# Layer 0's first shift columns: x loaded first, and four K tiles on TensorE instead of two there and two on VectorE

## Chip, cores and metric

The kernel runs on one core of a Trainium2 chip. The metric is the device time of one execution in microseconds (us), the median of several runs. The engines are TensorE (PE in the profile, its weight loads PEld), VectorE (DVE), ScalarE (ACT), GpSimd (POOL) and SyncE (SP), whose queue issues most of the loads.

## What is computed

Two blocks of two layers each, on x of 256 rows and 2048 columns, all in float32. The change is in the very beginning of layer 0 of the first block:

```python
mod = jax.nn.silu(c) @ w_mod + b_mod          # c: 2048, w_mod: 2048 x 6144
shift, scale, gate = jnp.split(mod, 3, axis=-1)
h = rms_norm(x, g_pre) * (1.0 + scale[:, None, :]) + shift[:, None, :]
proj = h @ w_in
```

Behind it come mixers (window attention, spatial gating, gated linear attention), the output projection, and a second block with attention and an MLP. None of that is touched.

## The kernel before

The 2048 columns of x are 16 K tiles of 128. The projection `h @ w_in` of layer 0 runs in four phases of four K tiles each, so that phase 0 can begin when scale and shift of only K tiles 0 to 3 are known; those of later K tiles come as background work on VectorE during the phase ahead. The diff is in the code that makes scale and shift for K tiles 0 to 3, ahead of phase 0. Everything there is the prologue.

There are two ways of multiplying the vector sc = silu(c) with a piece of w_mod. `gemv` (L488 to L501) loads tiles of 128 x 1024 (`raw`, two rows of K by 512 columns, or four by 256), scales each piece by one column of sc and adds it into `gacc` on VectorE (the first step is L494, the others L496), and at the end sums gacc over its 128 partitions with one matmul against a column of ones for each K tile (L501). `gemv_pe` (L522, L526) loads 128 x 8 x 128 tiles and multiplies on TensorE: for each K tile of the result two raw tiles and 16 matmuls with a 128 x 128 weight load and one moving column. All raw tiles come from one ring of five buffers, which the tiles of w_in use as well, so a load waits until the tile five places ahead has been used up. `mod_done` (L510, L512) adds the bias, and for the scale the gain.

In source order the kernel begins with four steps of the scale's gemv and four of gemv_pe for the shift of K tiles 0 and 1, one after the other, then transposes small vectors (`fill_fm`, L173), runs the rest of the scale, loads x (`x_load`, L154), squares it on ScalarE (`x_done`, L390), and runs gemv for the shift of K tiles 2 and 3. `block1` then makes 1/rms (L239, POOL L241, ACT L770, PE L771, copy L773), transposes x (L750), multiplies with scale (L754, VectorE) and adds the shift: the hi part of h is written by L762 on ScalarE and its remainder by L763 on VectorE; K tile 3 is kept whole by L758. Each weight tile of w_in is split the same way (L265 on ScalarE makes hi, L266 on VectorE makes lo), and TensorE multiplies three times (L287, L288, L289), or once where the K tile is whole (L325).

The order in which each engine gets its instructions is not the source's: the framework that builds the program interleaves independent work. Each engine then works through its own list in order, and one instruction that waits holds up all behind it. Where an instruction stands is therefore read from the built program.

Of the kernel before, what the change touches and what calls it, by code (L numbers as in the profile page):

```python
# [11 lines left out]
F32 = mybir.dt.float32  # L12
# [9 lines left out]
P = 128  # L22
S = 256
D = 2048
KT = D // P
# [65 lines left out]
def kernel(  # L91
# [7 lines left out]
    V, A, PE, G = nc.vector, nc.scalar, nc.tensor, nc.gpsimd  # L99

    const = ctx.enter_context(tc.tile_pool(name="const", bufs=1))
# [14 lines left out]
    def tm(tag, shape=(P, 512), dt=F32):  # L116
        return ring.tile(list(shape), dt, tag=tag, bufs=BUFS[tag], name=f"{tag}{next(uid)}")
# [10 lines left out]
    def gate_load(t, on):  # L128

        V.tensor_copy(out=t[0:1, 0:1], in_=on)  # L130

    def bank(pool=None, shape=(P, 512)):
        pool = pool or aux
        return pool.tile(list(shape), F32, tag="b", name=f"b{next(uid)}")
# [13 lines left out]
    def x_load(src, on=None):  # L148
        for n in range(4):
            for t in range(2):  # L150
                X[t][n] = tm("act")
                if on is not None:
                    gate_load(X[t][n], on)
                nc.sync.dma_start(out=X[t][n], in_=src[t * P:(t + 1) * P, n * 512:(n + 1) * 512])  # L154
# [25 lines left out]
    def fill_fm(on):  # L180
        fm_load(1, [both("bmod", b_mod), both("gpre", g_pre)], on)
        fm_load(2, [both("gpost", g_post), both("an", attn_norm_2), both("mn", mlp_norm_2), both("qn", q_a_norm_2),
                    both("kvn", kv_a_norm_2)], on)
# [75 lines left out]
    def raw_tile(tag="raw"):  # L259
        return wp.tile([P, 1024], F32, tag=tag, bufs={"raw": 5, "rawm": 2}[tag], name=f"{tag}{next(uid)}")  # L260
# [33 lines left out]
    def settle(age=0):  # L294

        while late and bg["n"] - late[0][0] >= age:
            late.pop(0)[1]()
# [87 lines left out]
    def x_done(t, n):  # L385

        if n == 0:
            ssx[t] = small(4)
        j = junk
        A.activation(out=j, in_=X[t][n], func=AF.Square, accum_out=ssx[t][:, n:n + 1])  # L390
# [82 lines left out]
    mod = {}  # L473
    idle = itertools.cycle(["k", "pT", "k", "s"])

    def gemv(l, part, k0, nk, eng, tag, into=None):

        if (l, part) not in mod:
            mod[l, part] = const.tile([P, KT], F32, name=f"mod{l}_{part}")
        n = nk * P  # L480
        per = 1024 // n
        if tag == "idle":
            per = 1
        n0 = part * D + k0 * P
        acc = gacc.tile([P, 1024], F32, tag="gacc", name=f"gacc{next(uid)}")[:, :n]
        for u in range(0, KT, per):
            raw = tm(next(idle)) if tag == "idle" else raw_tile(tag)
            nc.sync.dma_start(  # L488
                out=raw[:, :per * n].rearrange("p (k n) -> p k n", k=per),
                in_=w_mod[l, u * P:(u + per) * P, n0:n0 + n].rearrange("(k p) n -> p k n", p=P))  # L490
            for k in range(per):
                w = raw[:, k * n:(k + 1) * n]
                if u + k == 0:
                    eng.tensor_scalar(out=acc, in0=w, scalar1=sc[:, 0:1], scalar2=None, op0=MUL)  # L494
                else:
                    eng.scalar_tensor_tensor(out=acc, in0=w, scalar=sc[:, u + k:u + k + 1], in1=acc, op0=MUL, op1=ADD)  # L496
            if u + per == KT:
                def finish():
                    pb = bank(fin) if into is None else into
                    for i in range(nk):  # L500
                        PE.matmul(pb[:, i:i + 1], lhsT=acc[:, i * P:(i + 1) * P], rhs=ones[:, 0:1],  # L501
                                  start=True, stop=True)
                    if into is None:
                        mod_done(l, part, k0, nk, pb)
                late.append((bg["n"], finish))
            yield

    def mod_done(l, part, k0, nk, pb):
        o = mod[l, part][:, k0:k0 + nk]
        V.tensor_tensor(out=o, in0=pb[:, :nk], in1=fv(("bmod", l), part * KT + k0, nk), op=ADD)  # L510
        if part == 1:
            V.scalar_tensor_tensor(out=o, in0=o, scalar=1.0, in1=fv(("gpre", l), k0, nk), op0=ADD, op1=MUL)  # L512
        elif part == 2:
            V.tensor_tensor(out=o, in0=o, in1=fv(("gpost", l), k0, nk), op=MUL)

    def gemv_pe(l, part, k0, nk, tag, pb):

        for i in range(nk):
            n0 = part * D + (k0 + i) * P
            for u in range(0, KT, 8):  # L520
                raw = raw_tile(tag)
                nc.sync.dma_start(  # L522
                    out=raw.rearrange("p (k n) -> p k n", k=8),
                    in_=w_mod[l, u * P:(u + 8) * P, n0:n0 + P].rearrange("(k p) n -> p k n", p=P))
                for k in range(8):
                    PE.matmul(pb[:, i:i + 1], lhsT=raw[:, k * P:(k + 1) * P], rhs=sc[:, u + k:u + k + 1],  # L526
                              start=(u + k == 0), stop=(u + k == KT - 1))
                yield
# [726 lines left out]
    def mods(l, part, *ranges, eng=V, tag="rawm"):  # L1255
        return [gemv(l, part, k0, nk, eng, tag) for k0, nk in ranges]

    def run(gens):
        for g in gens:
            for _ in g:  # L1260
                pass
        settle()
# [25 lines left out]
    UN0 = 9  # L1288
    UN1 = 24
    RATE1 = 48  # L1290
    NPE = 2
    RATE0 = 31
    SPLIT0 = ("q0", "q1", "kv", "z0", "z1", "su", "sv", "z3", "qk", "v0", "v1")
    WHOLE0 = (3, 7, 11, 14, 15)
    pb = bank()
    scale, shift = mods(0, 1, (0, 4), tag="raw")[0], gemv_pe(0, 0, 0, NPE, "raw", pb)
    for i in range(4):
        next(scale)
        next(shift, None)
    fill_fm(None)  # L1300
    run([scale])
    x_load(x[0])
    for n in range(4):
        for t in range(2):
            x_done(t, n)
    run([gemv(0, 0, NPE, 4 - NPE, V, "raw", pb[:, NPE:])])
    mod_done(0, 0, 0, 4, pb)
    mask1 = const.tile([P, 512], F32, tag="mask", name="mask1")[:, :S]
    nc.gpsimd.dma_start(out=mask1, in_=cst[:, C_SWA:C_SWA + S])
    if N1:  # L1310
        block1(0, [(0,), (4,), (8,), (12,)], SPLIT0, ORDER, prepare0, lambda: None, WHOLE0)
    if N1 > 1:
# [61 lines left out]
```

## Time and profile before

| | us |
|---|---|
| median of 3 runs | 3034.97 (3031.36 to 3038.36) |
| profiled execution | 3032.83 |
| its span, first to last instruction | 3031.1 |
| TensorE busy in the span | 2944.8 |
| VectorE busy | 1985.4 |
| ScalarE busy | 1439.4 |
| first projection matmul (L287) starts | 50.31 |

The profile is one execution. A row of its timeline has the start, the length and the engine of a run of like instructions, with xN for N records. The profile records each float32 matmul of the prologue twice, so that the eight matmuls of one `gemv_pe` tile are x16. A matmul group's mean duration is longer than the pace at which they follow each other, because they overlap; so a run is read by its length, not by count times mean.

### The profile page before, as it was taken

The numbers are of one execution on the slowest core, as the hardware profiler recorded it, in microseconds if no ns is written. First come the engines' busy times: TensorE is split into PE (matmuls) and PEld (weight loads), VectorE is DVE, ScalarE is ACT, GpSimd is POOL, SyncE is SP. The second block draws the span as 40 slices with busy tenths as digits, with TensorE's granted clock in tenths as the row PEclk, the third lists the DMA queues.
The fourth block names the chain that finished last, engine by engine and source line by source line (L and its number), as shares of the span: only waits on it lengthen the run. The fifth ranks groups of instructions, "written<-read, shape, count | busy, mean of one in ns | idle before, by whom it ended". The sixth has DMA issues, their size and how long they took to land.

```text
span 3031.1 us, 40011 instructions
## 1 busy us (share of the span) xinstructions
PE 2944.8 (97%) x15002; PEld 2437.6 (80%) x15002; DVE 1985.4 (66%) x2832; ACT 1439.4 (47%) x2273; POOL 37.5 (1%) x56
## 2 busy tenths in 40 slices
PE   6999998999999999999999999999999999999998
PEld 5776676778787887888888888888788888888887
DVE  6898877678866565565666655665555655656655
ACT  2334545445556555544444444455554444444444
POOL 0000000000000000000000000000000000000000
PEclk9999998999999999999999999999999999999999
DMA  9998678888455555566666666554556666656664
GB/s 296 331 305 298 186 262 268 289 278 280 134 180 143 178 146 171 181 188 191 191 189 189 191 189 190 190 173 134 167 170 201 192 189 188 192 189 190 189 191 153
DMA packets 318838, 617.55 MB, mean 204 GB/s; under 512 B 21000, under 2 KB 48836, under 8 KB 318644
## 3 DMA queue, kind: packets, MB, share of 16 engines
q1 hardware_dynamic: 317988, 614.40, 64.2%
q8 instruction: 117, 1.92, 0.3%
q0 software_dynamic: 336, 0.49, 0.1%
q14 instruction: 77, 0.63, 0.1%
q10 hardware_dynamic: 320, 0.12, 0.0%
HBM read 610.73 MB, written 4.19 MB: 203 GB/s over the span
## 4 chain that ended last, share of the span: by engine, by line
PE 86%; DMA 6%; DVE 5%; ACT 2%; issue 1%; POOL 0%; SPq 0%; ACTq 0%; POOLq 0%; DVEq 0%
PE b L288 17%; PE b L289 17%; PE b L287 17%; PE b L1193 16%; PE b L1195 8%; DMA rawm<-in_w_mod_dram 4%; PE b L325 2%; DVE gacc L496 1%; PE b L366 1%; DVE lo L266 1%; PE b L567 1%; ACT hi L265 1%; PE b L554 1%; PE b L955 1%; PE b L501 0%
## 5 line engine op out<-in xcount | busy, mean ns | idle before, releaser
L266 DVE TENSOR_TENSOR lo<-raw,hi 128x1024 fp32r<-128x1024 f32 (+4 forms) x964 | 1126.2, 1170 | 798.2 <-ACT hi L265 794.8
L265 ACT CAST hi<-raw 128x1024 fp32r<-128x1024 f32 (+4 forms) x964 | 972.8, 1010 | 1284.8 <-PE b L289 783.8
L287 PE MATMUL b<-hi,act 128*128 128x512 f32 (+2 forms) x2728 | 1074.1, 394 | 4.6 <-ACT hi L265 2.2
L288 PE MATMUL b<-lo,act 128*128 128x512 f32 (+2 forms) x2728 | 1048.4, 384 | 8.7 <-DVE lo L266 8.7
L289 PE MATMUL b<-hi,act 128*128 128x512 f32 (+2 forms) x2728 | 1044.2, 383 | 0.4 <-DVE act L252 0.4
L1193 PE MATMUL b<-act,hi 128*128 128x512 f32 x2048 | 721.0, 397 | 0.0
L288 PEld LDWEIGHTS b<-lo,act 128*128 128x128 f32 x2728 | 515.7, 189 | 119.7 <-DVE lo L266 14.3
L287 PEld LDWEIGHTS b<-hi,act 128*128 128x128 f32 x2728 | 515.5, 189 | 115.1 <-issue 14.9
L289 PEld LDWEIGHTS b<-hi,act 128*128 128x128 f32 x2728 | 515.2, 189 | 97.3 <-issue 0.8
L1195 PE MATMUL b<-act,lo 128*128 128x256 f32 x2048 | 574.9, 281 | 0.0
L1193 PEld LDWEIGHTS b<-act,hi 128*128 128x128 f32 x2048 | 384.4, 188 | 92.7
L1195 PEld LDWEIGHTS b<-act,lo 128*128 128x128 f32 x2048 | 386.9, 189 | 0.5
L496 DVE SCALAR_TENSOR_TENSOR gacc<-rawm,sc,gacc 128x1024 f32<-128x1024 f32 x120 | 153.6, 1280 | 51.6 <-DMA rawm<-in_w_mod_dram 51.4
L325 PE MATMUL b<-raw,act 128*128 128x512 f32 (+1 forms) x240 | 110.3, 559 | 0.0
L1211 DVE SCALAR_TENSOR_TENSOR act<-b,s,act 128x512 f32<-128x512 f32 x128 | 90.0, 743 | 5.7 <-PE b L289 5.7
L354 ACT ACTIVATE s<-s,s 128x128 f32<-128x128 f32 (+3 forms) x144 | 64.1, 447 | 38.9 <-DVE s L351 37.8
L241 POOL TENSOR_TENSOR s<-s,cs 128x1 f32<-128x1 f32 (+1 forms) x38 | 28.6, 755 | 2892.7 <-DVE s L239 2806.0
L325 PEld LDWEIGHTS b<-raw,act 128*128 128x128 f32 x240 | 43.4, 189 | 17.9 <-issue 12.0
L1203 DVE SCALAR_TENSOR_TENSOR h<-h 128x256 f32<-128x256 f32 x128 | 54.5, 426 | 4.4
L390 ACT ACTIVATE junk<-act 128x512 bf16<-128x512 f32 x56 | 35.0, 626 | 42.8 <-DMA act<-in_x_dram 22.8
L824 DVE TENSOR_TENSOR act<-b,act 128x512 f32<-128x512 f32 (+2 forms) x82 | 51.5, 631 | 5.9 <-PE b L325 4.9
L1201 DVE TENSOR_TENSOR h<-b,h 128x256 f32<-128x256 f32 x128 | 53.4, 417 | 0.0
(272 smaller groups left out, 1725.9 us busy)
## 6 DMA issues: line engine op xcount, KB each, us to landing
raw<-in_w_in_dram SPq DMA_DIRECT2D x256, 512.0 KB, 4.7
raw<-in_w_up_dram SPq DMA_DIRECT2D x256, 512.0 KB, 3.7
raw<-in_w_down_dram SPq DMA_DIRECT2D x256, 512.0 KB, 3.6
rawm<-in_w_mod_dram SPq DMA_DIRECT2D x128, 512.0 KB, 4.8
raw<-in_w_out_dram SPq DMA_DIRECT2D x64, 512.0 KB, 4.8
raw<-in_w_o_dram SPq DMA_DIRECT2D x64, 512.0 KB, 3.7
k<-in_w_mod_dram SPq DMA_DIRECT2D x48, 256.0 KB, 4.9
raw<-in_w_in_dram SPq DMA_DIRECT2D x32, 288.0 KB, 2.9
```

The source lines that it names most:

```text
L265: A.copy(out=hi[:, :n], in_=src)
L266: V.tensor_tensor(out=lo[:, :n], in0=src, in1=hi[:, :n].bitcast(F32), op=SUB)
L287: PE.matmul(ps, lhsT=xa, rhs=wh, start=first, stop=False)
L288: PE.matmul(ps, lhsT=xa, rhs=wl, start=False, stop=False)
L289: PE.matmul(ps, lhsT=xb, rhs=wh, start=False, stop=last)
L325: PE.matmul(ps[t][:, :n], lhsT=a[:, t * P:(t + 1) * P], rhs=wh, start=kk + j == units[0], stop=kk + j == units[-1] + 3)
L354: A.activation(out=s[:, h, :], in_=s[:, h, :], func=AF.Exp, bias=nm[:, h:h + 1], accum_out=den[:, h:h + 1])
L496: eng.scalar_tensor_tensor(out=acc, in0=w, scalar=sc[:, u + k:u + k + 1], in1=acc, op0=MUL, op1=ADD)
L1193: PE.matmul(ps[f], lhsT=wh[:, f * P:(f + 1) * P], rhs=a.rearrange("p a b -> p (a b)"), start=(kk + j == 0), stop=False)
L1195: PE.matmul(ps[f][:, S:], lhsT=wl[:, f * P:(f + 1) * P], rhs=a[:, 0, :], start=False, stop=(kk + j == KT - 1))
L1203: V.scalar_tensor_tensor(out=s2, in0=s, scalar=0.0, in1=s, op0=MAX, op1=MUL)
L1211: V.scalar_tensor_tensor(out=xc, in0=ps, scalar=r2[t], in1=xc, op0=MUL, op1=ADD)
```

## The change

x_load goes to the front of SyncE's queue. The scale's gemv is no longer interleaved with gemv_pe, and stands whole behind fill_fm. The shift of all four K tiles is made by gemv_pe, behind the scale in the source, and the gemv of K tiles 2 and 3 is gone.

```diff
-    NPE = 2
     RATE0 = 31
...
+    x_load(x[0])
     pb = bank()
-    scale, shift = mods(0, 1, (0, 4), tag="raw")[0], gemv_pe(0, 0, 0, NPE, "raw", pb)
-    for i in range(4):
-        next(scale)
-        next(shift, None)
     fill_fm(None)
-    run([scale])
-    x_load(x[0])
+    run(mods(0, 1, (0, 4), tag="raw"))
     for n in range(4):
         for t in range(2):
             x_done(t, n)
-    run([gemv(0, 0, NPE, 4 - NPE, V, "raw", pb[:, NPE:])])
+    run([gemv_pe(0, 0, 0, 4, "raw", pb)])
+    if (0, 0) not in mod:
+        mod[0, 0] = const.tile([P, KT], F32, name="mod0_0")
     mod_done(0, 0, 0, 4, pb)
```

On TensorE the list of the kernel before begins with these rows (raw are the weight tiles, gacc the scale's sum, act the tiles of x):

```order
L526 MATMUL b_101<-sc,raw_108 128x1 x8
L173 MATMUL b_163<-cs,y_160 128x128
L173 MATMUL b_172<-cs,y_166 128x104
L526 MATMUL b_101<-sc,raw_122 128x1 x8
L526 MATMUL b_101<-sc,raw_136 128x1 x8
L526 MATMUL b_101<-sc,raw_150 128x1 x8
L750 MATMUL b_276<-cs,act_198 128x128
L501 MATMUL b_191<-cs,gacc_103 128x1 x4
```

All four L526 tiles stand ahead of L501. In the changed kernel the same place reads:

```order
L501 MATMUL b_167<-cs,gacc_134 128x1 x4
L526 MATMUL b_117<-sc,raw_184 128x1 x8
L771 MATMUL b_280<-h_281,cs 128x128
L771 MATMUL b_280<-h_284,cs 128x128
...
L526 MATMUL b_117<-sc,raw_214 128x1 x8
L526 MATMUL b_117<-sc,raw_224 128x1 x8
L526 MATMUL b_117<-sc,raw_234 128x1 x8
L526 MATMUL b_117<-sc,raw_244 128x1 x8
L526 MATMUL b_117<-sc,raw_254 128x1 x8
```

All eight tiles now stand behind L501; in the rows left out are two more of them, raw_194 and raw_204, and L750, L425 and L208. L501 itself still waits for the last VectorE step of the scale.

On ScalarE the list of the kernel before has, at the end of the prologue (mod_0 is the shift):

```order
L770 ACTIVATE h_271<-cs,s_265 128x128
L265 CAST hi_309<-raw_307 128x1024
L265 CAST hi_327<-raw_325 128x512
L265 CAST hi_357<-raw_355 128x1024
L762 ACTIVATE act_283<-h_281,mod_0_224 128x256
L762 ACTIVATE act_288<-h_286,mod_0_224 128x256
```

and the changed kernel:

```order
L770 ACTIVATE h_284<-cs,s_278 128x128
L762 ACTIVATE act_296<-h_294,mod_0_264 128x256
L762 ACTIVATE act_301<-h_299,mod_0_264 128x256
L762 ACTIVATE act_311<-h_309,mod_0_264 128x256
L758 ACTIVATE act_316<-h_314,mod_0_264 128x256
L265 CAST hi_322<-raw_320 128x1024
```

The casts of the first weight tiles moved from ahead of the instructions that wait for mod_0 to behind them. On VectorE the list of the kernel before has around mod_0 (gacc_339 is background work for the next phase):

```order
L494 TENSOR_SCALAR gacc_339<-k_340,sc 128x512
L496 SCALAR_TENSOR_TENSOR gacc_225<-raw_244,sc,gacc_225 128x256
L496 SCALAR_TENSOR_TENSOR gacc_339<-pT_343,sc,gacc_339 128x512
L496 SCALAR_TENSOR_TENSOR gacc_225<-raw_244,sc,gacc_225 128x256
L496 SCALAR_TENSOR_TENSOR gacc_339<-k_346,sc,gacc_339 128x512
L510 TENSOR_TENSOR mod_0_224<-b_101,fm 128x4
L266 TENSOR_TENSOR lo_358<-raw_355,hi_357 128x1024
```

and the changed kernel:

```order
L510 TENSOR_TENSOR mod_0_264<-b_117,fm 128x4
L763 SCALAR_TENSOR_TENSOR act_296<-h_294,mod_0_264,act_296 128x256
L763 SCALAR_TENSOR_TENSOR act_301<-h_299,mod_0_264,act_301 128x256
L763 SCALAR_TENSOR_TENSOR act_311<-h_309,mod_0_264,act_311 128x256
L266 TENSOR_TENSOR lo_323<-raw_320,hi_322 128x1024
L266 TENSOR_TENSOR lo_341<-raw_338,hi_340 128x512
L494 TENSOR_SCALAR gacc_352<-k_353,sc 128x512
```

The sixteen steps of the shift (here gacc_225) are gone, and the first splits and the first background steps moved from ahead of mod_0's L510 to behind it.

## Rows read from the trace of the kernel before

**Rows 1.** The page: busy time of TensorE, and its busy tenths in 40 slices.
```profile
PE 2944.8 (97%) x15002; PEld 2437.6 (80%) x15002; DVE 1985.4 (66%) x2832; ACT 1439.4 (47%) x2273; POOL 37.5 (1%) x56
...
PE   6999998999999999999999999999999999999998
```

**Rows 2.** Windows: start:end length, busy time by engine, granted clock, DMA share, GB/s.
```profile
0.00:10.00 10.00, 0.26 (x1) 0.18 (x1) 1.54 (x4) 1.50 (x2) 2.50 (x8) 1.00 0.76 202
10.00:20.00 10.00, 9.68 (x46) 9.62 (x46) 4.26 (x8) 0.00 (x0) 0.51 (x1) 1.00 0.89 274
20.00:30.00 10.00, 5.71 (x26) 5.34 (x27) 6.63 (x9) 1.44 (x4) 0.00 (x0) 1.00 0.97 327
30.00:40.00 10.00, 4.71 (x19) 3.59 (x19) 4.45 (x16) 5.14 (x14) 1.18 (x2) 1.00 1.05 346
40.00:50.00 10.00, 3.68 (x15) 3.13 (x16) 9.45 (x22) 3.18 (x5) 0.00 (x0) 1.00 1.01 350
...
50.00:90.00 40.00, 40.00 (x172) 30.32 (x171) 31.92 (x55) 17.71 (x33) 0.00 (x0) 1.00 0.90 310
```

**Rows 3.** Timeline 0 to 32: start, length, engine, line, tiles, records [idle before].
```profile
10.07 3.54 PE L526 MATMUL b<-sc,raw 128*128 128x1 f32 x16 [5.65 <-DMA raw<-in_w_mod_dram]
...
13.64 0.37 SPq L522 DMA_DIRECT2D raw<-in_w_mod_dram  x1
...
17.60 6.99 PE L526 MATMUL b<-sc,raw 128*128 128x1 f32 x32 [0.25 <-DMA raw<-in_w_mod_dram]
...
23.03 6.26 DVE L496 SCALAR_TENSOR_TENSOR gacc<-raw,sc,gacc 128x512 f32<-128x512 f32 x8 [2.41 <-DMA raw<-in_w_mod_dram]
...
29.35 1.87 PE L501 MATMUL b<-cs,gacc 128*128 128x1 f32 x8 [0.80 <-DVE gacc L496]
```

**Rows 4.** Timeline 40 to 52: the first cast, mod_0 and the first projection matmul.
```profile
40.95 1.05 ACT L265 CAST hi<-raw 128x1024 fp32r<-128x1024 f32 x1 [4.56 <-DMA raw<-in_w_in_dram]
...
43.76 1.22 DVE L266 TENSOR_TENSOR lo<-raw,hi 128x1024 fp32r<-128x1024 f32 x1
...
48.28 1.01 PE L501 MATMUL b<-cs,gacc 128*128 128x1 f32 x4 [4.94 <-DVE gacc L496]
...
49.33 0.16 DVE L510 TENSOR_TENSOR mod<-b,fm 128x4 f32<-128x4 f32 x1 [0.45 <-PE b L501]
...
49.53 1.31 ACT L762 ACTIVATE act<-h,mod 128x256 fp32r<-128x256 f32 x3 [2.02 <-DVE mod L510]
...
50.31 0.78 PE L287 MATMUL b<-hi,act 128*128 128x512 f32 x1
...
50.74 0.49 ACT L758 ACTIVATE act<-h,mod 128x256 f32<-128x256 f32 x1
...
51.31 0.63 PE L287 MATMUL b<-hi,act 128*128 128x512 f32 x1
...
51.74 0.63 PE L289 MATMUL b<-hi,act 128*128 128x512 f32 x1
```

**Rows 5.** Groups by line and form, 0 to 51 or 55: busy, mean ns, idle before.
```profile
L526 PE MATMUL b<-sc,raw 128*128 128x1 f32 x64 | 14.0, 351 | 5.9 <-DMA raw<-in_w_mod_dram 5.9
...
L496 DVE SCALAR_TENSOR_TENSOR gacc<-raw,sc,gacc 128x256 f32<-128x256 f32 x15 | 7.2, 480 | 0.1
L750 PE MATMUL b<-cs,act 128*128 128x128 f32 x20 | 5.5, 431 | 3.9 <-DMA act<-in_x_dram 3.5 <-DVE mod L510 0.3 <-DVE sgb L209 0.2
...
L771 PE MATMUL b<-h,cs 128*128 128x128 f32 x4 | 1.6, 502 | 3.7 <-ACT h L770 3.7
```

**Rows 6.** Timeline at 140 us: an L501 of four K tiles between projection matmuls.
```profile
140.26 0.95 PE L501 MATMUL b<-cs,gacc 128*128 128x1 f32 x8
```

**Rows 7.** The raw tiles up to 50 us: duration ns min/median/max, first and last start.
```profile
L526 PEld LDWEIGHTS b<-sc,raw x64: 288/333/338, 10.0 to 24.2; 128*128 128x128 f32 x64
```

**Rows 8.** A window at the end of a phase, columns as in rows 2.
```profile
140.00:150.00 10.00, 8.72 (x50) 7.07 (x49) 8.64 (x18) 3.33 (x4) 0.00 (x0) 1.00 0.84 271
```

## The prediction

> **What bounds the kernel now.** I read first the busy time of each engine and the span in slices: TensorE is busy 97% of the span, and of the 40 slices only the first falls clearly under nine tenths [rows 1]. So over most of the span nothing but fewer TensorE seconds helps, and the change touches none of those; what it can move is the first slice. The windows over that slice say where its idle time is: TensorE works 0.26, 9.68, 5.71, 4.71 and 3.68 us in the five stretches of 10 us up to 50, and 40.00 of 40 from 50 to 90 [rows 2]. The change therefore moves one number, the moment at which the first projection matmul (L287) starts. It starts at 50.31 us [rows 4], and a shift of it should pass to the end nearly whole, because behind it TensorE hardly waits for anything that could soak it up.
>
> What ends that prologue is read from the timeline. VectorE finishes the scale half at 29.29 (the run of eight L496 that starts at 23.03 and takes 6.26), and L501 folds it at 29.35 [rows 3]. The shift of K tiles 2 and 3 is then worked off on VectorE: sixteen steps, of which the 15 L496 of the 256-column form take 7.2 us [rows 5], spread over 35 to 48 between other work; L501 folds them at 48.28, L510 makes mod_0 at 49.33, ScalarE makes the first h tile from 49.53, and L287 follows [rows 4]. The four tiles of shift that TensorE computes (L526) run from 10.07 to 24.6, wholly beside the loads and VectorE work of the scale half [rows 3]: today they cost nothing.
>
> **What the change takes away.** The sixteen VectorE steps and the L501 of 1.01 us behind them go. In windows 30 to 50 VectorE was busy 4.45 and 9.45 us of ten [rows 2]; that is relief on the chain that ends the prologue now.
>
> **What it adds.** Eight tiles of L526 instead of four. The program's tile is eight matmuls, which the profile records as 16 rows; one tile took 3.54 us, the two that run back to back 6.99, and all four 14.0 of busy time [rows 3, 5]. So 3.50 us a tile, 28.0 us for eight.
>
> **What it moves, and this decides.** In the order of the changed program all eight tiles stand on TensorE behind the L501 of the scale half. L501 waits for the whole scale half, so none of the 28.0 us can run beside it any more; what cost nothing is now in line. The cover is lost, and nothing new covers it: between the eight tiles stand only L771, the L750 transposes and the three little transposes, and they add to the line too.
>
> **The sum.** When does L501 start? The bytes ahead of the last scale tile are the same as before: 2.1 MB of shift tiles were ahead of it, now 2.1 MB of x, with 4.2 MB of scale. So it is not later than 29.35 [rows 3]. The gain is that SyncE's queue no longer stands still for TensorE's tiles (the transfer issued at 13.64 is one that waited until the first L526 tile was done [rows 3]). At the highest rate of the prologue, 350 GB/s [rows 2], 6.3 MB take 18.0 us, and with the first issue at 1.7 and one last pair of steps of 1.57 (6.26 / 4) that is 21.3 at the earliest. At the rates that the windows had, 202 then 274 then 327 GB/s, 2.0 MB are in by 10, 4.8 MB by 20 and 6.3 MB by 24.7, plus 1.57: 26.3. I take 26.3, since these are this program's own rates at its start. From there, in program order on TensorE: L501 1.87 [rows 3] gives 28.2; eight tiles 28.0 give 56.2; L771 1.6 [rows 5] gives 57.8; twelve of the L750 stand in the line (four are ahead of L501, four beside the work behind mod_0) and three smaller transposes, fifteen at the 5.5 / 20 = 0.275 of an L750 [rows 5], 4.1, gives 61.9. Then 0.20 to mod_0, as between the end of L501 at 49.29 and that of L510 at 49.49 [rows 4]: 62.1.
>
> Behind mod_0 the order on ScalarE changes too. Before, the first cast of weights (L265) was done at 42.0, long ahead [rows 4]; now it stands behind the three L762 and the L758. These took from 49.53 to 51.23 [rows 4], 1.74 with the step to them, and the cast 1.05: 64.9 for the first L287, against 50.31, so **14.6 us later**. The low half (L266, 1.22 [rows 4]) then waits for that cast, while before it was done at 45; two L287 at the starting pace of 0.43 (51.31 to 51.74 [rows 4]) cover 0.86 of it, so 0.4 more. The four background steps (L494 and three L496, up to 6.26 / 8 = 0.78 each [rows 3]) that VectorE did ahead of phase 0 now lie inside it. VectorE is busy 31.92 of 40 us there [rows 2], which leaves room; they cost nothing if the room is where they fall and 3.1 if all of them end up ahead of a waiting matmul, as the end of a phase shows it can happen (TensorE idles 1.28 us from 140 to 150 [rows 8]). I take 0.5, nearer to the lower end, since 8 us of the 40 are free.
>
> 14.6 + 0.4 + 0.5 = 15.5. The profiled execution took 3032.83, with 1.7 of it outside the span: 3048.3. It stands 2.1 below the median of the three runs, 3034.97; I put half of that on top: **3049 us, slower by 0.5%**.
>
> **Rivals.** *The long stretch runs at full speed.* The granted clock says 1.00, the level of 2.4 GHz, for every window of the prologue [rows 2], but by their durations the instructions there ran as at the lower of the two levels, 1.2 GHz: the weight load of L526 took 333 ns as a median [rows 7], and the eight records of an L501 took 1.87 us at 29.35 [rows 3] but 0.95 at 140.26, between projection matmuls [rows 6]. At that pace a tile takes 16 x 0.95 / 8 = 1.9, eight take 15.2, L501 0.95: 13.7 less in the line, first L287 at about 51.2, the end within 0.2% of today. Against it: over 14.0 us of work between 10.07 and 24.6 the pace of 0.22 us a record (3.54 / 16) did not change, the last pair of tiles being as slow as the first [rows 3, 5]. 0.09. Beside this: the Trainium skill, TensorE: Matmul & The Clock Gate, section Part 1: The HAM clock gate, says that the throttled state is the default and that sustained matmul activity releases it. By that rule the 28 us would speed up on the way and the sum would be this rival's; the trace does not agree for this kind of matmul, a 128x128 weight load for one column, which stayed slow to its end.
>
> *Faster.* The same mechanism with the rest going well: L501 at 21.3, tiles at the pace of the transfers, 524 kB / 350 GB/s = 1.5 us, 12.0 for eight, and L501, L771 and L750 at half their durations (0.95 + 0.8 + 1.65), 0.4 for the little ones: 37.1, plus 0.2, 1.74 and 1.05: 40.1, and 0.9 for the later terms, 9 us early: 3023. All terms but the start and the tiles are 7.7 there (0.95 + 0.8 + 1.65 + 0.4 + 0.2 + 1.74 + 1.05 + 0.9), so it turns to faster where a tile costs less than (50.31 - 21.3 - 7.7) / 8 = 2.7 with that early start, and less than 2.0 with a start at 26.3. For it speaks that 7 us of VectorE steps are gone and x is squared long before it is wanted; against it the 3.50 of all four tiles. 0.04.
>
> *Only half the tiles are exposed.* If x and the scale come in faster than I think, or part of the tiles run before L501, the loss is smaller: with L501 at 21.3 the sum is 10.5, 3043. That is the lower part of my own case, and the order on TensorE leaves no tile ahead of L501. *More in phase 0:* with L501 at 29.3 and all 3.1 of background steps exposed, 15.5 + 3.0 + 2.6 = 21.1, 3054 to 3056. That is its upper part.
>
> **How the numbers follow.** My case 0.87, the clock rival 0.09, faster 0.04. The ends of my own case are 3043 and 3056; a clock that rises half way through the tiles would take 6 to 7 us off, to 3042, and the three runs before spread from 3.6 below their median to 3.4 above. That makes 3039 to 3058, with some 2 in 10 outside, most of them in the clock rival. About 0.2% (6 us) is what a measurement of this kernel can tell from no change: slower by more than that 0.86, within it 0.10 (the clock rival, and a little of the low end), faster 0.04.
>
> **What would show it.** The timeline of the changed kernel should have L501 at 25 to 28, then 128 records of L526 in some 28 us with only L771, L750, L425 and L208 between them, mod_0 near 62, the first cast behind L762, and L287 at 63 to 67; TensorE's busy time should be about 13 us higher (four tiles more, one L501 less), and the stretch behind L287 unchanged in length. It is wrong if L526 takes under 0.15 us a record, if tiles run ahead of L501, or if L287 starts before 57; if L287 starts near 65 and the end is not 13 us later, the belief that a shift passes whole to the end was wrong.

## The result, and the profile after

The changed kernel takes 3054.5 us (median of 3 runs, 3053.47 to 3059.07) against 3034.97: 1.0072 times as long, with a 95% interval of 1.0056 to 1.0088, so 17 to 27 us slower. The profiled execution spans 3052.8 us, 21.7 more than before. The prediction was slower, 3049, with 3039 to 3058 as its range.

The first loss stands in the timeline of the changed kernel (start, length, engine, line, tiles, records, idle before and what ended it); it answers [rows 3] and [rows 4]:

```profile
17.14 10.98 DVE L496 SCALAR_TENSOR_TENSOR gacc<-raw,sc,gacc 128x512 f32<-128x512 f32 x14
...
28.17 1.87 PE L501 MATMUL b<-cs,gacc 128*128 128x1 f32 x8 [18.43 <-DVE gacc L496]
...
29.90 3.55 PE L526 MATMUL b<-sc,raw 128*128 128x1 f32 x16
...
34.95 3.41 PE L526 MATMUL b<-sc,raw 128*128 128x1 f32 x16
...
38.91 3.57 PE L526 MATMUL b<-sc,raw 128*128 128x1 f32 x16
...
44.38 17.07 PE L526 MATMUL b<-sc,raw 128*128 128x1 f32 x80
...
61.48 0.16 DVE L510 TENSOR_TENSOR mod<-b,fm 128x4 f32<-128x4 f32 x1 [18.59 <-PE b L526]
61.67 1.31 ACT L762 ACTIVATE act<-h,mod 128x256 fp32r<-128x256 f32 x3 [42.94 <-DVE mod L510]
...
63.29 2.50 ACT L265 CAST hi<-raw 128x1024 fp32r<-128x1024 f32 x3
...
64.37 1.22 PE L287 MATMUL b<-hi,act 128*128 128x512 f32 x2 [1.56 <-ACT hi L265]
...
65.63 0.80 PE L288 MATMUL b<-lo,act 128*128 128x512 f32 x1
```

TensorE waits 18.43 us for the scale, and only then do the eight L526 tiles run, 27.6 us of them, with hardly anything beside them. ScalarE had waited 42.94 us when mod_0 came, and the first cast stands behind its work. The first L287 is 14.06 us later than before.

The windows of the same stretch, with the columns of [rows 2], say it without a single instruction: TensorE has nothing to do from 10 to 20, and from 40 to 60 it is all but the only engine with work (VectorE has 0.17 us), while the transfers fall to 119 GB/s. The granted clock of 1.00 in these rows is not a reading of the speed; the last section says why.

```profile
10.00:20.00 10.00, 0.00 (x0) 0.00 (x0) 4.36 (x11) 4.35 (x12) 1.97 (x2) 1.00 1.01 342
20.00:30.00 10.00, 1.83 (x9) 1.83 (x9) 7.76 (x11) 0.00 (x0) 0.00 (x0) 1.00 1.03 314
30.00:40.00 10.00, 10.00 (x48) 9.75 (x48) 2.57 (x8) 0.00 (x0) 0.00 (x0) 1.00 0.56 149
40.00:50.00 10.00, 10.00 (x49) 9.96 (x49) 0.17 (x1) 0.00 (x0) 0.00 (x0) 1.00 0.43 119
50.00:60.00 10.00, 10.00 (x48) 10.00 (x49) 0.00 (x0) 0.00 (x0) 0.00 (x0) 1.00 0.71 226
```

The rest is lost between 64 and 126: 10.2 us, of which 7.6 are left at the end. The starts of the same matmuls in both kernels show where (a chunk is a slice of w_in's columns, up to 512 wide; v1 is one of them):

| start of | before | after | later by |
|---|---|---|---|
| first L287 | 50.31 | 64.37 | 14.06 |
| first L325, end of the first chunk | 55.06 | 70.59 | 15.53 |
| last L325 of chunk v1 | 80.72 | 96.26 | 15.54 |
| last L325 of phase 0 | 92.01 | 112.69 | 20.68 |
| second L325 of phase 1 | 101.45 | 125.68 | 24.23 |
| first matmul of L955, second block | 1058.5 | 1080.7 | 22.2 |

Nothing is lost while the chunks run on (70 to 96). The loss comes in two places where VectorE has other work ahead of the splits. There the changed kernel's timeline has these idle times, and its windows these granted clocks (the sixth number behind the window's length, not counting those in brackets, ahead of the DMA share):

```profile
98.34 0.73 PE L287 MATMUL b<-hi,act 128*128 128x512 f32 x2 [0.69 <-ACT hi L265]
...
100.77 0.79 PE L288 MATMUL b<-lo,act 128*128 128x512 f32 x1 [1.70 <-DVE lo L266]
...
114.67 1.02 PE L501 MATMUL b<-cs,gacc 128*128 128x1 f32 x8 [0.52 <-DVE gacc L496]
...
118.25 0.80 PE L288 MATMUL b<-lo,act 128*128 128x512 f32 x1 [1.99 <-DVE lo L266]
```

```profile
100.00:102.00 2.00, 1.24 (x3) 1.05 (x4) 2.00 (x5) 1.04 (x1) 0.00 (x0) 0.60 1.05 399
102.00:104.00 2.00, 2.00 (x6) 1.55 (x6) 1.93 (x8) 0.00 (x0) 0.00 (x0) 0.55 1.06 389
...
118.00:120.00 2.00, 1.75 (x4) 1.47 (x5) 2.00 (x6) 1.08 (x2) 0.00 (x0) 0.50 0.33 63
120.00:122.00 2.00, 2.00 (x6) 1.52 (x6) 1.93 (x4) 0.00 (x0) 0.00 (x0) 0.50 0.99 342
122.00:124.00 2.00, 2.00 (x7) 1.52 (x6) 1.09 (x1) 0.00 (x0) 0.00 (x0) 0.50 0.68 259
```

So 4.9 us of waiting, and from the second wait of each pair on the clock is at its lower level, 1.2 GHz (0.50), for some microseconds in which TensorE, once the wait is over, is busy all the time. That costs some 4.5 us of work more: half of the 9 us or so that it works at that level. What stands ahead of the two late splits on VectorE:

```profile
99.41 0.17 DVE L413 TENSOR_SCALAR s<-s 128x16 f32<-128x16 f32 x1
99.49 1.22 DVE L266 TENSOR_TENSOR lo<-raw,hi 128x1024 fp32r<-128x1024 f32 x1
...
113.77 0.75 DVE L496 SCALAR_TENSOR_TENSOR gacc<-s,sc,gacc 128x512 f32<-128x512 f32 x1
...
115.81 1.26 DVE L754 SCALAR_TENSOR_TENSOR h<-b,mod,rb 128x256 f32<-128x256 f32 x3
116.98 1.22 DVE L266 TENSOR_TENSOR lo<-raw,hi 128x1024 fp32r<-128x1024 f32 x1
```

The first split stands behind small steps of the next phase (the rope tables); the second behind the last background step, which ends at 114.5, and the L754 that follow it there. The kernel before waits 0.2 us in the same phases, at a granted clock of 1.00 throughout (the timeline, then the window over them):

```profile
99.56 0.50 PE L288 MATMUL b<-lo,act 128*128 128x512 f32 x1 [0.18 <-DVE lo L266]
```

```profile
53.00:115.00 62.00, 61.72 (x263) 44.96 (x262) 52.65 (x102) 29.68 (x52) 0.00 (x0) 1.00 0.95 336
```

### The profile page after: what moved, and what is told of

It reads as the page before. It is cut to its first block, busy times and chain, and to the rows that moved or that the text cites. A ratio compares the mean times of both kernels' runs of the same rounds, so it can differ in the third digit from the quotient of the medians.

```text
span 3052.8 us, 40106 instructions
## 1 busy us (share of the span) xinstructions
PE 2963.4 (97%) x15062; PEld 2456.1 (80%) x15062; DVE 1981.1 (65%) x2816; ACT 1437.3 (47%) x2273; POOL 38.0 (1%) x56
## 4 chain that ended last, share of the span: by engine, by line
PE 85%; DVE 5%; DMA 5%; ACT 2%; issue 2%; POOL 0%; SPq 0%; ACTq 0%; DVEq 0%; POOLq 0%
PE b L288 17%; PE b L289 17%; PE b L287 17%; PE b L1193 16%; PE b L1195 8%; DMA rawm<-in_w_mod_dram 4%; PE b L325 2%; DVE gacc L496 2%; DVE lo L266 1%; PE b L366 1%; PE b L526 1%; PE b L567 1%; ACT hi L265 1%; PE b L501 1%; PE b L955 1%
## 5 line engine op out<-in xcount | busy, mean ns | idle before, releaser
L266 DVE TENSOR_TENSOR lo<-raw,hi 128x1024 fp32r<-128x1024 f32 (+4 forms) x964 | 1126.9, 1171 | 804.1 <-ACT hi L265 800.9
L265 ACT CAST hi<-raw 128x1024 fp32r<-128x1024 f32 (+4 forms) x964 | 971.6, 1009 | 1265.2 <-PE b L289 777.6
L287 PE MATMUL b<-hi,act 128*128 128x512 f32 (+2 forms) x2728 | 1076.1, 395 | 4.9 <-ACT hi L265 3.0
L288 PE MATMUL b<-lo,act 128*128 128x512 f32 (+2 forms) x2728 | 1051.6, 386 | 11.2 <-DVE lo L266 11.2
L288 PEld LDWEIGHTS b<-lo,act 128*128 128x128 f32 x2728 | 517.8, 190 | 121.8 <-DVE lo L266 16.2
L287 PEld LDWEIGHTS b<-hi,act 128*128 128x128 f32 x2728 | 517.1, 190 | 117.7 <-issue 16.4
L325 PE MATMUL b<-raw,act 128*128 128x512 f32 (+1 forms) x240 | 111.3, 563 | 0.0
L325 PEld LDWEIGHTS b<-raw,act 128*128 128x128 f32 x240 | 44.2, 192 | 18.6 <-issue 12.5
L1201 DVE TENSOR_TENSOR h<-b,h 128x256 f32<-128x256 f32 x128 | 53.5, 418 | 0.0
L257 DVE TENSOR_TENSOR act<-h,act 128x256 fp32r<-128x256 f32 x128 | 50.9, 419 | 0.0
```

Source lines behind the costliest of these rows:

```text
L265: A.copy(out=hi[:, :n], in_=src)
L266: V.tensor_tensor(out=lo[:, :n], in0=src, in1=hi[:, :n].bitcast(F32), op=SUB)
L287: PE.matmul(ps, lhsT=xa, rhs=wh, start=first, stop=False)
L288: PE.matmul(ps, lhsT=xa, rhs=wl, start=False, stop=False)
L325: PE.matmul(ps[t][:, :n], lhsT=a[:, t * P:(t + 1) * P], rhs=wh, start=kk + j == units[0], stop=kk + j == units[-1] + 3)
```

## The experiments

All were compared with runs of the kernel before on the same chip; ratios are to those, with a 95% interval. Single runs of the kernel before spread by some 10 us either way, so a profile's span alone settles little, and the starts inside the trace are read beside the ratio.

### One part alone: x first

```diff
+    x_load(x[0])
     pb = bank()
...
     run([scale])
-    x_load(x[0])
```

> One part of the change alone: x is loaded first, everything else as before (two K tiles of shift on TensorE interleaved with the scale, two on VectorE). My theory, that the loss is only the eight L526 tiles that lost their cover, gives no loss here: the tiles stay ahead of L501, and since x is squared and folded early the VectorE half of the shift is no longer interleaved with L754 and waits for its loads alone: mod_0 near 40, first L287 at 41 to 45 us against 50.3, time 6 to 9 us under the kernel before (ratio about 0.998). The rival, that x ahead of the weights is itself what costs (7 us of transfers in front of the first raw tile), gives a first L287 at 55 or later and at least 5 us more than before.

Measured: 1.0020 (1.0007 to 1.0033), first L287 at 56.80. My theory falls. The rival holds for the first L287; whether the whole costs its 5 us, the interval of 2 to 10 us leaves open. The rows of this kernel:

```profile
18.02 3.55 PE L526 MATMUL b<-sc,raw 128*128 128x1 f32 x16 [9.81 <-DMA raw<-in_w_mod_dram]
...
21.85 1.10 PE L771 MATMUL b<-h,cs 128*128 128x128 f32 x4
...
25.80 3.57 PE L526 MATMUL b<-sc,raw 128*128 128x1 f32 x16
...
30.12 6.83 PE L526 MATMUL b<-sc,raw 128*128 128x1 f32 x32
```

```profile
20.00:30.00 10.00, 8.48 (x41) 8.06 (x41) 5.46 (x11) 0.00 (x0) 0.56 (x1) 1.00 0.48 146
```

The first L526 starts 8 us later than before (18.02 against 10.07 [rows 3]), since the raw tiles now queue behind x; and the list of TensorE has L771, transposes and L208, which waits 1.52 us for a small load, ahead of the second tile, so that tile ends late, its buffer is not free, and SyncE's queue stands 7.3 us for it: from 20 to 30 the transfers make 146 GB/s, against 327 before [rows 2]. L501 comes at 42.34. In the changed kernel this cost does not show at L501, since there no raw tile waits for TensorE ahead of it: its L501 came at 28.17, 1.2 earlier than before.

### The other part alone: four K tiles on TensorE, interleaved

```diff
-    NPE = 2
+    NPE = 4
-    for i in range(4):
+    for i in range(8):
         next(scale)
         next(shift, None)
...
-    run([gemv(0, 0, NPE, 4 - NPE, V, "raw", pb[:, NPE:])])
```

> The other part alone: four K tiles of shift on TensorE, but interleaved tile by tile with the scale, and x loaded after them as before. My theory: the eight L526 tiles then run beside the scale from 10 us on, 28 us of them end near 39 to 40, 7 us of transposes and L771 behind them, first L287 at 46 to 48: 2 to 5 us under the kernel before. The rival, that four K tiles on TensorE cost their 14 us more wherever they stand, gives a first L287 at 60 to 64 and a time 10 us or more over the kernel before.

Measured: 1.0003 (0.9989 to 1.0016), first L287 at 49.31, later than the 46 to 48 expected and 1.0 earlier than before. Thirty-two matmuls more on TensorE (64 records), at 3.5 us a tile as before, cost nothing at that point when seven of the eight tiles stand beside the scale:

```profile
26.87 10.40 PE L526 MATMUL b<-sc,raw 128*128 128x1 f32 x48 [0.78 <-DMA raw<-in_w_mod_dram]
...
37.42 1.87 PE L501 MATMUL b<-cs,gacc 128*128 128x1 f32 x8 [0.15 <-DVE gacc L496]
...
39.15 3.55 PE L526 MATMUL b<-sc,raw 128*128 128x1 f32 x16
...
45.19 1.54 PE L771 MATMUL b<-h,cs 128*128 128x128 f32 x4 [1.54 <-ACT h L770]
...
49.31 0.80 PE L287 MATMUL b<-hi,act 128*128 128x512 f32 x1 [1.32 <-ACT act L762]
```

The tiles end at 42.7, and what is late next is x, whose squares start at 38. The rival, that four tiles cost their 14 us wherever they stand, falls. The gain of 2 to 5 us in the time that I expected did not come: this kernel, too, loses at the entry of phase 1 (its second L325 there is at 108.91, 7.5 later than before, with a single wait of 3.5 us for L266 on the way).

### Both parts, with the tiles interleaved

Against the changed kernel:

```diff
+    NPE = 4
...
     pb = bank()
+    scale, shift = mods(0, 1, (0, 4), tag="raw")[0], gemv_pe(0, 0, 0, NPE, "raw", pb)
+    for i in range(8):
+        next(scale)
+        next(shift, None)
     fill_fm(None)
-    run(mods(0, 1, (0, 4), tag="raw"))
+    run([scale])
...
-    run([gemv_pe(0, 0, 0, 4, "raw", pb)])
```

> Both parts of the change, x first and four K tiles of shift on TensorE, but the shift interleaved with the scale as in the kernel before, so that seven of the eight L526 tiles stand ahead of L501. My theory: L526 from 14 us on, 28 us of tiles and about 6 us of L750 and L771 between them, the end of the tiles near 46 to 48, first L287 near 49 to 51: within 3 us of the kernel before, some 18 us under the changed kernel. The rival, that the place of the tiles does not matter, gives the changed kernel's 64 us and 3054.

Measured: 1.0034 (1.0021 to 1.0046), first L287 at 56.1. Better than the changed kernel by 8 us at that point, but not the 49 to 51 expected, and 6 to 14 us over the kernel before where 3 were expected: the first L526 starts at 18.5, as with x first alone. Both effects are there, the place of the tiles and the cost of x ahead of the raw ring.

### Half of the disputed work

```diff
-                for k in range(8):
+                for k in range(0, 8, 2):
```

> The changed kernel with every second matmul of each L526 tile left out (so the shift is not the right one); loads, order and waits stay. It takes half of the disputed cost away. Theory: L526 14 us instead of 28, first L287 at 50 to 51 instead of 64.4, and 13 to 15 us less in all: 3039 to 3041, since what the changed kernel loses behind the first L287 (some 7 us) is another thing and stays. Rival one: transfers are late too, so the line shortens by less, first L287 at 55 or later. Rival two: the loss behind the first L287 hangs on the late start, and goes with it: 3033.

Measured: 1.0047 (1.0028 to 1.0065), first L287 at 52.34, 12.03 earlier than in the changed kernel:

```profile
29.80 1.87 PE L501 MATMUL b<-cs,gacc 128*128 128x1 f32 x8 [19.75 <-DVE gacc L496]
31.53 1.84 PE L526 MATMUL b<-sc,raw 128*128 128x1 f32 x8
...
40.88 8.53 PE L526 MATMUL b<-sc,raw 128*128 128x1 f32 x40
```

The tiles take 13.95 us (1.84, 1.71, 1.87 and 8.53 for five), half of 27.6, and the rest is that L501 comes at 29.80 in this execution, 1.6 later. So the line shortens one for one. The second loss stays: the second L325 of phase 1 comes at 112.95, 11.5 later than before, where the first L287 was only 2.0 later, with the same two kinds of wait. So it does not hang on how late the start is. The total came out higher than the 3039 to 3041 expected; its interval of 8 to 20 us over the kernel before cannot say by how much.

### The small steps at the entry of phase 1

```diff
     elif p == 1:
-            fill_rope()
-            fill_vectors()
...
+    fill_rope()
+    fill_vectors()
     run([gemv_pe(0, 0, 0, 4, "raw", pb)])
```

> The changed kernel with the rope tables (fill_rope: L427, L430, L412 to L457) and the two little gate vectors made in the prologue, where VectorE is idle, instead of at the entry of phase 1. It tests the second loss of the changed kernel, some 7 us behind its first L287. Theory: at 98 to 104 us the first split of the next chunk (L266) stands on VectorE behind a dozen of these small steps, TensorE waits 0.69 and 1.70 us there and then works at a granted clock of 0.55 to 0.60; without the steps the wait at 100 and the low clock behind it go, first L287 stays at 64 to 65, and the time falls by 2 to 5 us, to 3050 to 3053. Rival: the loss comes from the background steps (L496) alone, and nothing changes within 1 us. Second rival: the steps only move the wait to the prologue, first L287 2 us later.

Measured: 1.0071 (1.0053 to 1.0089), no gain. Of the theory only this holds: the wait of 1.70 us for L266 at 100 becomes 0.52. ScalarE's 0.69 stays, the low clock behind them stays (0.50 from 102 to 104), and at the entry of phase 1 another wait of 1.73 for ScalarE's cast appears. The second rival is the one that fits. The small steps now stand among the steps of the scale on VectorE, which is not idle there, so L501 comes 2.3 later, and so does the first L287, at 66.65:

```profile
30.50 1.86 PE L501 MATMUL b<-cs,gacc 128*128 128x1 f32 x8 [17.83 <-DVE gacc L496]
```

Behind the first L287 2.5 us less are lost: the second L325 of phase 1 is at 125.46, against 125.68.

### The pace of L526 after dense work

```diff
+    wb = bank(fin)
+    for _ in range(22):
+        PE.matmul(wb, lhsT=ident, rhs=X[0][0], start=True, stop=True)
     run(mods(0, 1, (0, 4), tag="raw"))
```

> The changed kernel with 22 dense matmuls (128x512 float32, into a bank that nobody reads) on the idle TensorE between about 7 and 27 us, so that it arrives at L501 and the L526 tiles out of 20 us of dense work. It measures the disputed cost, the pace of L526. If sustained work had been all that L526 lacked, L501 takes 0.95 and each tile 1.7 to 1.9 us to the end, and the first L287 starts at 50 to 52: some 13 us less than the changed kernel. My theory: L501 and perhaps the first tile run fast, then the tiles fall back to 3.5 us each, since they did not speed up themselves in 28 us; first L287 at 60 to 63.

Measured: 3061.45 us, first L287 at 61.85. It is a single run, so its time settles nothing, but its trace is the clearest picture of the disputed cost (timeline, then windows with the granted clock; L1299 is the dense work):

```profile
13.92 14.77 PE L1299 MATMUL b<-act,cs 128*128 128x512 f32 x34
...
28.97 0.95 PE L501 MATMUL b<-cs,gacc 128*128 128x1 f32 x8
29.78 1.92 PE L526 MATMUL b<-sc,raw 128*128 128x1 f32 x16
...
32.98 3.57 PE L526 MATMUL b<-sc,raw 128*128 128x1 f32 x16
...
41.86 17.07 PE L526 MATMUL b<-sc,raw 128*128 128x1 f32 x80
```

```profile
28.00:32.00 4.00, 4.00 (x34) 3.61 (x33) 0.69 (x3) 0.00 (x0) 0.00 (x0) 1.00 1.16 293
32.00:34.00 2.00, 2.00 (x14) 1.79 (x13) 1.67 (x5) 0.00 (x0) 0.00 (x0) 0.69 1.07 273
34.00:60.00 26.00, 25.75 (x121) 25.51 (x121) 1.12 (x6) 0.84 (x3) 0.00 (x0) 0.50 0.60 185
```

Out of 20 us of dense matmuls L501 takes 0.95 and the first tile 1.92, at the level of 2.4 GHz; then the granted clock falls to 0.50, 1.2 GHz, although TensorE is busy 2.00 of 2 us there and 25.75 of the 26 behind, and the tiles take 3.57 and 17.07 for five, as in the changed kernel without dense work. My theory holds. The rule that I weighed in the prediction, from the Trainium skill, TensorE: Matmul & The Clock Gate, section Part 1: The HAM clock gate (sustained matmul activity releases the throttle), fits the dense matmuls here, whose first ten records take 7.32 us and the next 34 take 14.77. For the L526 tiles this trace does not bear it out: the clock fell while TensorE worked through them and did not rise again in their 26 us.

### Two versions meant to be faster

Against the interleaved kernel (the same two calls are gone from phase 1):

```diff
     run([scale])
+    fill_rope()
+    fill_vectors()
     x_load(x[0])
```

> Four K tiles of shift on TensorE interleaved with the scale, x behind them, and the rope tables in the prologue. If the 6 to 7 us that the interleaved kernel without the early tables loses between 80 and 110 us (3.5 us of waiting for L266 and a low granted clock) come from those steps, this one keeps the first L287 at 49 to 50 and its first L325 of phase 1 comes at 100 to 103 instead of 107.4: 3 to 6 us under the kernel before, 3028 to 3033 on its 3035. Otherwise it equals the kernel before within 2 us, or the small steps between the scale's L496 delay the raw ring and the first L287 comes at 51 or later.

Measured: 1.0014 (1.0000 to 1.0028), first L287 at 53.5. It lost 4.4 us ahead of the second tile, where TensorE now waits for a small load that GpSimd issues (L208 for sg_b), which pushes the L526 tiles back. The first L325 of phase 1 comes at 106.96, not at 100 to 103: behind its first L287 this kernel loses 4.6 us less than the interleaved one, and about as much ahead of it. With x moved up between the pairs:

```diff
         next(shift, None)
+        if i == 1:
+            x_load(x[0])
```

> As the interleaved kernel with early rope tables, but x is loaded behind the second pair of weight tiles, not first and not last. Theory: the queue does not stand in front of an L771 that waits for x, as it did with x first (TensorE idle from 12 to 18 us there), and the transposes fall between tiles; TensorE is then the bound of the prologue, 28 us of L526 and some 9 us of the rest from 10 us on, first L287 at 47 to 50, 3 to 6 us under the kernel before. Rival: L771 stands in the list ahead of the fourth tile and waits for the squares, so the ring stalls again and the first L287 comes at 52 to 56.

Measured: 1.0037 (1.0022 to 1.0053), first L287 at 56.30. The rival is right: L771 waits 2.86 us for L770, which needs the squares of x, until 30.60, behind the same 4.7 us for L208, and the eight tiles end at 53.6.

### Where the second loss comes from

```diff
-            background(mods(0, 1, (4, 4), tag="idle") + mods(0, 0, (4, 4), tag="idle"), 32 / UN0)
+            for part in range(2):
+                V.tensor_copy(out=mod[0, part][:, 4:8], in_=mod[0, part][:, 0:4])
```

The same edit in the changed kernel:

> The changed kernel without the background work of phase 0 (scale and shift of K tiles 4 to 7 are copied from those of K tiles 0 to 3 instead of computed, so the output is another one; 64 L494 and L496 steps and their loads are gone). To be read against the kernel before with the same left out. It asks where the second loss of the changed kernel, some 8 us between 96 and 126 us, comes from. Theory: VectorE is crowded there because the background lies further behind, so without it the waits for L266 of 1.70 and 1.99 us and the low clock behind them go, and the pair differs by the prologue's 14 to 16 us alone. Rival: the waits come from the order of ScalarE's and VectorE's lists at the entry of phase 1 whatever the background, and the pair differs by 20 us or more.

and in the kernel before:

> The kernel before with the background work of phase 0 left out in the same way (K tiles 4 to 7 take a copy of scale and shift of K tiles 0 to 3). It is the other half of the pair. Its first L287 should be at 47 to 50, since VectorE has three background steps less between the shift's steps; its time should be within 3 us of the kernel before, which hardly waits in phase 0.

Measured: 1.0060 (1.0043 to 1.0077) and 1.0014 (1.0000 to 1.0028). The traces of the pair run in step: first L287 at 65.2 and 50.9, last L325 of phase 0 at 109.01 and 95.10, second L325 of phase 1 at 115.29 and 101.37, 13.9 apart at the end as at the beginning. They differ by 12.6 us in the medians and 9.7 in the spans of the two traces. In the changed kernel without background no wait of TensorE is left between 70 and 130, and the clock stays up:

```profile
96.00:104.00 8.00, 8.00 (x37) 5.84 (x36) 6.25 (x18) 4.19 (x9) 0.00 (x0) 1.00 0.91 315
104.00:112.00 8.00, 8.00 (x35) 5.93 (x34) 7.34 (x26) 3.97 (x9) 0.00 (x0) 1.00 0.98 345
112.00:120.00 8.00, 8.00 (x33) 5.74 (x31) 7.85 (x14) 5.07 (x9) 0.00 (x0) 1.00 1.00 334
```

So the second loss needs the background work of phase 0 (its steps on VectorE or its loads, which went too; the waits of TensorE end at a split, a cast or a background step, none at a load); without it only the prologue's 14 us are left.

The other traces say more. Every version that keeps the background loses time between its first L287 and the second L325 of phase 1, measured against the kernel before: from 3.9 us (tiles interleaved, early rope tables) to 10.5 (both parts, interleaved), and 8.5 in the interleaved kernel, whose first L287 is 1.0 earlier than before. The two without background lose none. So this loss belongs to no late start and not to this change alone; the kernel before is the one order, of those tried with background, whose trace is free of it. The kernel before without it was expected within 3 us of itself with it, and its first L287 no later than 50; it came out 0 to 8 us slower and at 50.9, so taking work away from VectorE is no gain in that kernel.

### Dense matmuls between the tiles

```diff
+                PE.matmul(wb, lhsT=ident, rhs=raw[:, :512], start=True, stop=True)
                 yield
...
+    for _ in range(6):
+        PE.matmul(wb[:, :384], lhsT=ident, rhs=cs[:, :384], start=True, stop=True)
...
+        if i == 3:
+            x_load(x[0])
```

> Four K tiles of shift on TensorE, interleaved with the scale, x behind the fourth pair, and dense matmuls that nobody reads: six of 128x384 at the start and one of 128x512 behind each L526 tile. If dense work now and then keeps TensorE at its full speed, a tile with its dense matmul takes 2.6 to 2.8 us instead of 3.5, the eight end near 36 to 38 us, the transposes take half, and the first L287 comes at 43 to 46: 4 to 7 us under the kernel before. If not, each tile takes 3.5 and the dense matmul 1.7, 14 us more of TensorE, and the first L287 comes at 60 to 64 and the time at 3045 to 3050.

Measured: 1.0066 (1.0044 to 1.0088), first L287 at 55.22, in neither of the two ranges expected, and the time, 3049.95, at the end of the slower one. The first tile takes 1.92, the second 2.81, then 3.41 each with 2.05 for the dense one, and in the window 20 to 30 the granted clock is 0.50 with TensorE busy 10.00 of 10. The fifth tile is an exception: behind 3 us of transposes and the like it takes 2.02, and the next are slow again:

```profile
27.20 2.05 PE L528 MATMUL b<-raw,cs 128*128 128x512 f32 x2
...
32.05 2.02 PE L526 MATMUL b<-sc,raw 128*128 128x1 f32 x16
```

The dense matmuls do not hold the clock up here and cost more than they bring. No version beat the kernel before.

## Why the prediction was right, point by point

- *What bounds the kernel, and that a shift of the first L287 passes to the end.* Right as far as the runs can tell. With 14.06 us at the first L287 the span is 21.7 longer, and nothing between shows them soaked up. But single traces scatter on that way: from the second L325 of phase 1 to the end of the span the distance to the kernel before changes by -2.5 us here, by -10.4 with x first alone and by +9.9 in the kernel before without background. That a shift passes whole is shown only within such bounds. The sign that the stretch behind L287 stays unchanged in length failed: it is 7.6 us longer, which is the second loss.
- *The start of L501.* 26.3 forecast, 28.17 measured, inside its bounds of 21.3 and 29.35. That it is near is in part luck, since I had the wrong bound: the sum lets the transfers set the end of the scale. The raw tiles wait behind x, the first step on VectorE is at 15.70, and from there VectorE has sixteen steps to do; the last fourteen run without a pause and take 10.98 us. VectorE sets the time of L501, not the last transfer.
- *Eight tiles at 3.50.* 28.0 forecast, 27.6 measured; that they stand alone on the path is shown by the interleaved kernel, where they cost nothing at the first L287, and by the half tiles, which give back half.
- *The rest of the line.* From the start of L501 to the end of mod_0's L510 35.8 us forecast, 33.5 measured (61.64 - 28.17). L771 took 1.20, and the transposes overlap the tiles at their ends. The two misses cancel, which is luck: first L287 at 64.9 forecast, 64.37 measured.
- *The first split.* 0.4 forecast, and 0.4 measured: L288 starts 1.26 us behind the first of two L287, which cover 0.86. Not forecast was that the slow pace behind the first L287 lasts longer, to 69.6, 5 us behind the first L287 against 2.5 before; together they make about the 1.47 that the first chunk adds in the table.
- *The background on VectorE.* This is the term that was mis-sized: 0.5, with 3.1 as its bound; the table shows 8.7 between chunk v1 and phase 1, of which some 2 are no longer there at 1058. The place and the kind of cause were named, as the pair without background shows. The bound was wrong because it counted the four displaced steps by themselves. They cost nothing where they stood, at 66 to 68; what costs is the splits (L266) and casts (L265) that come late at two entries, 4.9 us, and then the granted clock, which falls at the second wait of each pair. A bound for a wait ahead of dense TensorE work has to contain the slow stretch behind it, about as much again here. The centre of the forecast is 5.5 us low for this reason. That the upper end of my own case, 21.1 us, lies so near the 21.7 measured is luck: it took L501 3.0 late and 3.1 for the background, and measured were 1.9 and 8.7, with 2.3 gained in the line.
- *The rivals.* The clock rival is refuted by the changed kernel itself, where no tile took under 3.4 us; the kernel with dense work ahead shows that a clock already up does not last through the tiles either. The rival on the other side, faster, needed tiles under 2.0 us, or 2.7 with the earliest start; of the whole tiles only those came near that ran while the clock was up in the two kernels with dense work. That x first costs time by itself was in none of them; the run with x first alone shows it.

What stays open: why the framework's order at the entry of phase 1 differs between the versions, and so which part of the 7 to 9 us is the order and which the crowded VectorE. The early rope tables changed the order and kept most of the loss; the pair without background changed both. There is one trace of each version, the kernel before included.

## What to carry to other kernels

Work on an engine that is idle is free only beside something else that is needed: before moving it, look in the built order at which instruction stands ahead of it and what that one waits for. A load moved to the front of a queue takes its place from the loads behind it, and if their buffers form a ring, whatever stands ahead of a buffer's consumer in that engine's list holds up the whole queue (7.3 us with x first alone). And a wait ahead of dense matmuls can cost more than its length: here 4.9 us of waits cost some 4.5 more at the lower clock.

## What the hardware showed that I had not expected

- The granted clock fell while TensorE was busy: behind 20 us of dense matmuls, L501, one L526 tile and some small matmuls still ran at 1.00; then the clock fell to 0.50, and the other seven L526 tiles, with a few small matmuls, followed at that level; from 34 to 60 TensorE was busy 25.75 us.
- The granted clock of 1.00 in the prologue rows [rows 2] is not a reading of the speed. In the kernel with dense work ahead the same L526 at the same 3.57 us a tile are recorded at 0.50. In the changed kernel the column stays at 1.00 from the start to the first fall, at 100, but up to 69.6 its projection matmuls follow each other every 0.43 us and from 69.9 on every 0.23: the first stretch was at 1.2 GHz. Only a trace in which the clock had risen earlier shows the tiles' level in the column.
- Two waits of together 2.4 us between 98 and 101, in an otherwise busy stretch, were followed by some 3 us at the lower level.
